# The first feed-forward product as seven half-size products, in a one-core block with three mixers

## The chip, the cores and the metric

The kernel runs on one core of one Trainium2 chip. The metric is device time in microseconds of one launch, the median of several runs.

## The reference, cut to what matters

One residual layer over 512 tokens of width 1024: three token mixers (gated DeltaNet, stick-breaking attention, gated short convolution), merged and projected, then a feed-forward part. All of it is float32. The change is in the feed-forward part:

```python
x = x + rms_norm(merged @ w_out[l], norm_mix_post[l])
h = rms_norm(x, norm_ffn_pre[l])                        # 512 x 1024
f = jnp.square(jax.nn.relu(h @ w_ff1[l])) @ w_ff2[l]    # 1024 -> 4096 -> 1024
x = x + rms_norm(f, norm_ffn_post[l])
```

## The kernel before, in words

**Precision.** Every matmul operand is split into a high part (rounded on ScalarE) and a low part (what remains, subtracted on VectorE), and a product takes three matmuls: high by high, high by low, low by high (`mm3`, L179). Weights come in units of 128 x 1024 numbers, 512 KB: a load on SP's queue into `raw`, a cast on ScalarE (L143), a subtraction on VectorE (L144), into one of three `hl` buffers. These steps are given an earlier place in the order than the work around them (`early`), and each load follows the load before (`lastw`).

**Order.** The program is written out by hand and a planner orders each engine's instructions by the given priorities. First come the projections (`proj`, one weight unit and 24 matmuls each), with the mixers' work put between them by `tick`. Then the output projection, with `out_norm` for each of the four token blocks (residual, norms, `x1` stored in DRAM for later) and `out_transpose`, which puts the normed block on its other axis, as high and low part `h2h`, `h2l`.

**First feed-forward product.** 32 columns of 128 outputs, each with 24 matmuls of 128 x 128 by 128 x 512 (`ff1_mm`). The first three columns are done in token halves, because the last two blocks are not transposed yet. `ff1_act` makes ReLU on ScalarE and multiplies by the sum itself on VectorE, into `aT` (one tile per token half and 256 outputs). `X` and `W` are differences of these tiles, used by the second product.

**Second feed-forward product.** It is already made of seven products of half size each way (Winograd's form of Strassen's scheme), called Q, R, Q, R, S, V, S in the code (`product`), on differences of the activations and on sums of the weights. The weight sums S5, S6 and S1 (8 units each) are made in DRAM, during earlier stages, by `presum`: one call issues on SP's queue a copy of a unit from DRAM to DRAM, and on GpSimd's queue the addition of another unit to the copy issued two calls earlier (`LAG`). Calls stand behind every second gate of the mixers' merge (4) and behind 24 columns of the first product. The last of the seven products adds a further unit in SBUF: a load on SP's queue into one of eight `ch` slots, then an adding transfer on GpSimd's queue (L988).

**Buffers.** PSUM has 8 banks: five of tag `c`, three of tag `mm`. SBUF has 64 tiles of 128 x 512 (`g2`), two of 16 KB a partition (`h16`, which hold h2h and h2l and later the `ch` slots).

## Time and profile before

| | |
|---|---|
| median of 3 runs | 904.28 us (903.99 to 904.78) |
| the profiled execution | 905.1 us |
| its span, first to last instruction | 903.4 us |
| TensorE, VectorE, ScalarE, GpSimd busy | 885.4, 589.0, 452.1, 105.8 us |
| mean granted clock of TensorE | 0.996 |
| moved by transfers | 137 MB |

The busy time of TensorE counts pipelined matmuls with modelled ends, so it says that TensorE had work, not that it ran at its peak. Times in the rows below are microseconds from the start of the span; the first feed-forward product runs from 564.8 to 742.6 us, the second from there to 893.

### The profile page before, as it was taken

Reading aid. Unit: us, or ns where it says so; the run is one execution under the profiler, and the core shown is the slowest. Engines: PE = TensorE matmul, PEld = TensorE weight load, DVE = VectorE, ACT = ScalarE, POOL = GpSimd, SP = SyncE. Lnnn points to the kernel's source line nnn. Section 1 sums busy time; section 2 is a strip of 40 time slices with the busy share of each in tenths; the row PEclk is TensorE's granted clock in tenths of the full one; section 3 lists DMA queues with packets and bytes.
Section 4 is the critical chain, followed back from the end, with each engine's and each line's share of the span. In section 5 each row is a group of like instructions: output and inputs, shape, how many; then the busy total and the mean of one; then the engine's idle time right before and its main releaser. Section 6 shows DMA issues by size and latency. Waiting matters only on the chain.

```text
span 903.4 us, 11761 instructions
## 1 busy us (share of the span) xinstructions
PE 885.4 (98%) x4224; PEld 736.7 (82%) x4224; DVE 589.0 (65%) x1026; ACT 452.1 (50%) x825; POOL 105.8 (12%) x165
## 2 busy tenths in 40 slices
PE   9999999999999999999999999999999999999996
PEld 7788888877788888888888878988888888888885
DVE  4885678987777659655565546533334459878886
ACT  6556875657787732233344333322223237566562
POOL 1003221010112120200000111011111000000120
PEclk9999999999999999999999999999999999999998
DMA  9322223222113144524243552299999339566692
GB/s 313 125 86 82 70 79 118 73 103 71 68 38 106 50 127 121 162 90 117 70 152 126 173 191 94 98 288 288 284 286 269 122 111 373 187 194 203 190 267 103
DMA packets 41626, 136.97 MB, mean 152 GB/s; under 512 B 5456, under 2 KB 5456, under 8 KB 41184
## 3 DMA queue, kind: packets, MB, share of 16 engines
q1 hardware_dynamic: 34032, 111.24, 35.2%
q0 software_dynamic: 7248, 24.68, 13.0%
q8 instruction: 33, 0.54, 0.2%
q10 hardware_dynamic: 288, 0.30, 0.1%
q14 instruction: 25, 0.20, 0.1%
HBM read 131.48 MB, written 29.88 MB: 179 GB/s over the span
## 4 chain that ended last, share of the span: by engine, by line
PE 83%; DVE 10%; issue 3%; ACT 3%; DMA 1%; POOL 0%; DVEq 0%; POOLq 0%; SPq 0%; ACTq 0%
PE mm L179 51%; PE Q L179 5%; PE R L179 5%; PE po L179 5%; PE S L179 5%; PE psv L179 2%; PE V L179 2%; DVE hl L144 2%; DVE c L682 2%; PE p L179 2%; DVE z L683 1%; DVE XX L513 1%; PE pg L179 1%; DVE XX L507 1%; PE warm L179 1%
## 5 line engine op out<-in xcount | busy, mean ns | idle before, releaser
L179 PE MATMUL mm<-hh,hl 128*128 128x512 f32 x928 | 306.0, 397 | 0.9 <-ACT ct L729 0.9
L143 ACT CAST hl<-raw 128x1024 fp32r<-128x1024 f32 x116 | 111.6, 962 | 217.7 <-PE mm L179 189.0
L144 DVE TENSOR_TENSOR hl<-raw,hl 128x1024 fp32r<-128x1024 f32 x116 | 129.9, 1120 | 138.1 <-ACT hl L143 137.8
L179 PEld LDWEIGHTS mm<-hh,hl 128*128 128x128 f32 x928 | 174.1, 188 | 35.7 <-ACT ct L729 1.3
L179 PE MATMUL mm<-hl,hl 128*128 128x512 f32 x464 | 181.1, 390 | 0.0
L179 PE MATMUL mm<-h2h,hl 128*128 128x512 f32 (+1 forms) x528 | 155.0, 377 | 0.4 <-ACT h2h L187 0.2
L179 PEld LDWEIGHTS mm<-h2h,hl 128*128 128x128 f32 x528 | 97.2, 188 | 18.8 <-ACT h2h L187 0.8
L179 PEld LDWEIGHTS mm<-hl,hl 128*128 128x128 f32 x464 | 87.5, 189 | 16.0
L179 PE MATMUL mm<-h2l,hl 128*128 128x512 f32 (+1 forms) x264 | 99.5, 377 | 0.1
L997 DVE TENSOR_TENSOR hl<-ch,hl 128x1024 fp32r<-128x1024 f32 x53 | 64.6, 1223 | 6.2 <-ACT hl L996 6.1
L179 PEld LDWEIGHTS mm<-h2l,hl 128*128 128x128 f32 x264 | 49.7, 188 | 9.4 <-DVE h2l L188 0.3
L996 ACT CAST hl<-ch 128x1024 fp32r<-128x1024 f32 x53 | 55.3, 1046 | 0.0
L179 PE MATMUL po<-wo,mg 128*128 128x512 f32 x192 | 45.2, 391 | 0.0
L179 PEld LDWEIGHTS po<-wo,mg 128*128 128x128 f32 x192 | 35.8, 188 | 7.9 <-ACT mg L187 0.3
L179 PE MATMUL Q<-hl,ahi 128*128 128x512 f32 x128 | 39.7, 391 | 0.0
L179 PE MATMUL R<-hl,ahi 128*128 128x512 f32 x128 | 39.4, 389 | 0.0
L168 POOL DMA_DIRECT2D S<-wst x24 | 20.0, 832 | 151.9 <-DMA S<-wst 115.4
L179 PE MATMUL S<-hl,ahi 128*128 128x512 f32 x120 | 37.0, 389 | 0.0
L682 DVE TENSOR_TENSOR_SCAN c<-c,w 128x512 f32<-128x512 f32 (+3 forms) x32 | 25.5, 815 | 15.1 <-ACT w L106 15.0
L187 ACT CAST ahi<-aT 128x512 fp32r<-128x512 f32 x32 | 19.8, 622 | 28.7 <-PE Q L179 12.1
L179 PEld LDWEIGHTS Q<-hl,ahi 128*128 128x128 f32 x128 | 24.0, 188 | 5.7 <-ACT hl L996 0.4
L947 DVE TENSOR_TENSOR aT<-r,mm 128x256 f32<-128x256 f32 x62 | 23.1, 413 | 7.7 <-ACT r L942 7.7
(297 smaller groups left out, 1448.7 us busy)
## 6 DMA issues: line engine op xcount, KB each, us to landing
raw<-wst SPq DMA_DIRECT2D x92, 512.0 KB, 3.3
ch<-S SPq DMA_DIRECT2D x32, 512.0 KB, 4.3
raw<-wst SPq DMA_DIRECT2D x48, 256.0 KB, 3.2
S<-wst POOLq DMA_DIRECT2D x24, 512.0 KB, 8.7
ch<-wst SPq DMA_DIRECT2D x21, 512.0 KB, 5.2
S<-wst SPq DMA_DIRECT2D x16, 512.0 KB, 8.6
S<-S SPq DMA_DIRECT2D x8, 512.0 KB, 8.7
ch<-wst POOLq DMA_DIRECT2D x8, 512.0 KB, 8.7
```

The lines of the kernel that those rows point to most:

```text
L143: nc.scalar.copy(hl[:, 0, :], raw)
L144: nc.vector.tensor_tensor(hl[:, 1, :], raw, rf(hl[:, 0, :]), ALU.subtract)
L168: nc.gpsimd.dma_start(t, wsrc(1024, *key), accum_op=ALU.add, max_dma_last_dim=4096)
L179: return nc.tensor.matmul(o, l, r, start=start, stop=stop, skip_group_check=more)
L187: nc.scalar.copy(hi, src)
L507: nc.vector.tensor_tensor(tmp[:, :, :w], X[:, :, j].unsqueeze(2).to_broadcast([P, 8, w]), L[:, j, j + 1:].unsqueeze(1).to_broadcast([P, 8, ...
L513: nc.vector.tensor_tensor(X[:, :, j + 1:], X[:, :, j + 1:], tmp[:, :, :w], ALU.subtract)
L682: nc.vector.tensor_tensor_scan(back, back, w[j][:, ks][:, ::-1], 0.0, ALU.add, ALU.add)
L683: nc.vector.tensor_tensor(z[j][:, :n], z[j][:, :n], c[j][:, :n], ALU.subtract)
L947: x = nc.vector.tensor_tensor(aT[i][u][:, f % 2, :], r[:, c], ps[:, c], ALU.mult)
L996: after[0] = nc.scalar.copy(hl[0][:, c], r)
L997: after[1] = nc.vector.tensor_tensor(hl[1][:, c], r, rf(hl[0][:, c]), ALU.subtract)
```

## The change

**The first product** becomes seven products of half size: tokens in halves, the 1024 inner numbers in halves (k), the 4096 outputs in halves (n). For each group u of 256 outputs there are M1 to M7, each 24 matmuls of 128 x 128 by 128 x 256 with one weight unit. The left operands are the quarters A(i, q) of h2 (token half i, inner half q) and four combinations X, Y, Z, W, made by `combine` on VectorE after the transposes and split in high and low parts. On the right, M2, M3 and M4 use plain units, M5 and M6 use the sums F5 and F6, made in DRAM by `presum`; M1 uses F5 plus one more unit, added in SBUF in one of two buffers, and M7 adds another unit to the sum that M1 left there. The results are added and subtracted on VectorE (`step`) and then go through ReLU and square as before.

**The order.** The lead is M5 of groups 0 and 1, which needs the plain quarter A(0, 0) only, then M3, M2, M1, M4, M6, M7 of both groups with the transposes of the last two token blocks in between. Groups 2 to 7 follow one after the other.

**Weight sums.** There are 32 sums in DRAM instead of 24: F5 and F6 are new, S1 goes. The calls of `presum` now stand in every second projection, but not while `quiet` is set (parts of the triangular inverse, and from the last gates to the output projection), and in every fourth of the seven-product steps. In the second feed-forward product the S product adds its second unit in SBUF slots, and the last product adds one more unit to these slots in place; V uses other buffers.

**Other.** `x1` is stored from GpSimd's queue instead of SP's.

```diff
-    S5, S6, S1 = ([dp.tile([P, 1024], F32, tag=f"{n}{u}", bufs=1, name=f"{n}{u}") for u in range(8)]
-                  for n in ("S5", "S6", "S1"))
+    def sums(which, n):
+        return [dp.tile([P, 1024], F32, tag=f"{which}{n}{u}", bufs=1, name=f"{which}{n}{u}") for u in range(8)]
...
+    def plan(t, of, plus):
...
+    def f1(k, n):
...
+    def f2(k, n):
...
+    F5, F6, S5, S6 = (sums(w, n) for w in "FS" for n in (5, 6))
+    plan(F5, f1(1, 1), f1(0, 1))
+    plan(F6, f1(0, 0), f1(0, 1))
+    plan(S5, f2(1, 1), f2(0, 1))
+    plan(S6, f2(0, 0), f2(0, 1))
+    quiet = [False]
+    calls = [0]
...
     def presum():
+        if quiet[0]:
+            return
...
     def proj(c0, x=False):
+        calls[0] += 1
+        if calls[0] > 2 and calls[0] % 2:
+            presum()
...
     def gdn_inverse(h0):
+        quiet[0] = True
...
+        quiet[0] = False
         for j in range(31):
+            quiet[0] = j >= 16
...
+        quiet[0] = False
...
-        if dm % 2 == 1:
-            presum()
...
+    quiet[0] = True
...
-    h2h = hp.tile([P, KT, T], F32R, tag="h16", name="h2h")
-    h2l = hp.tile([P, KT, T], F32R, tag="h16", name="h2l")
...
+    FB, op = {}, {}
+    homes = [hp.tile([P, 4, 4, 256], F32R, tag="h16", name=nm("h2")) for _ in range(2)]
+    for j, (p_, q_) in enumerate(((("A", 0, 0), "X"), (("A", 1, 0), ("A", 1, 1)))):
+        op[p_] = [[homes[j][:, e, 2 * g:2 * g + 2, :] for g in range(2)] for e in range(2)]
+        op[q_] = [[homes[j][:, 2 + e, 2 * g:2 * g + 2, :] for g in range(2)] for e in range(2)]
...
-            nc.sync.dma_start(x1d[b, hf], x1[hf])
+            nc.gpsimd.dma_start(x1d[b, hf], x1[hf])
...
     def out_transpose(b, h2):
-        bs = slice(b * P, b * P + P)
+        i, ts_ = b // 2, slice(b % 2 * P, b % 2 * P + P)
         for q in range(2):
             pt = bank("pt")
             for j in range(4):
                 nc.tensor.transpose(pt[:, j * P:j * P + P], h2[q][:, j * P:j * P + P], ident)
             p3 = pt.rearrange("p (k c) -> p k c", k=4)
-            split(h2h[:, q * 4:q * 4 + 4, bs], h2l[:, q * 4:q * 4 + 4, bs], p3)
+            if b % 2 == 0:
+                FB[i, q] = [g2("F", F32, (P, 2, 256)) for _ in range(2)]
+            if (i, q) == (0, 0):
+                split(homes[0][:, 0, :, ts_], homes[0][:, 1, :, ts_], p3)
+            elif i == 1:
+                split(homes[1][:, 2 * q, :, ts_], homes[1][:, 2 * q + 1, :, ts_], p3)
+            for g in range(2):
+                nc.scalar.copy(FB[i, q][g][:, :, ts_], p3[:, 2 * g:2 * g + 2, :])
+        if b % 2 == 0:
+            return
+        if i == 0:
+            FB["X"] = [g2("X", F32, (P, 2, 256)) for _ in range(2)]
+            combine("X", FB["X"], FB[0, 1], FB[0, 0])
+        else:
+            combine("Y", FB["X"], FB[1, 1], FB["X"])
+            combine("Z", FB[1, 0], FB[1, 0], FB["X"])
+            combine("W", FB[0, 1], FB[0, 1], FB[1, 1])
+    def combine(name, o, a=None, b=None):
+        if name not in op:
+            op[name] = [[g2("op", F32R, (P, 2, 256)) for _ in range(2)] for _ in range(2)]
+        for g in range(2):
+            if a is not None:
+                nc.vector.tensor_tensor(o[g], a[g], b[g], ALU.subtract)
+            split(op[name][0][g], op[name][1][g], o[g])
...
+    NR = 3
+    raws = [[(slice(0, 512), g2("rw")), (slice(512, 1024), g2("rw"))] for _ in range(NR)]
...
-    def ff1_mm(w, ps, ts_):
...
+    big = []
+    def slot(n):
+        if not big:
+            for _ in range(2):
+                t = hp.tile([P, 4, 1024], F32, tag="h16", name=nm("ch"))
+                big.extend([(all_, t[:, i, :])] for i in range(4))
+        return big[n % 8]
+    def right(src, raw, plus=None, second=True):
+        if raw is None:
+            raw = [(all_, wp.tile([P, 1024], F32, tag="raw", bufs=2, name=nm("raw")))]
...
-            lastw[0] = x
+            if src is not None:
+                x = nc.sync.dma_start(r, src[:, c])
+                dep(x, lastw[0])
+                lastw[0] = x
             if plus is not None:
                 nc.gpsimd.dma_start(r, plus[:, c], accum_op=ALU.add)
...
-    def block(k, n):
-        return lambda u: wsrc(1024, "ff2", n, 8 * k + u)
+    def block(k, n, slots):
+        return lambda u: (wsrc(1024, *f2(k, n)(u)), slots(u))
+    def m2_slot(u):
+        return raws[(2, 0, 1)[u]] if u < 3 else slot(u - 3)
+    m2_block = block(0, 0, m2_slot)
...
+    wsum = {"M1": F5, "M5": F5, "M6": F6, "M2": f1(0, 0), "M3": f1(1, 1), "M4": f1(1, 0)}
+    more = {"M1": f1(0, 0), "M7": f1(1, 0)}
+    left = {"M1": "Y", "M2": ("A", 1, 0), "M3": "X", "M4": ("A", 1, 1), "M5": ("A", 0, 0), "M6": "Z", "M7": "W"}
+    done = [0]
+    def ff1_product(m, ps, u, first):
+        done[0] += 1
+        if done[0] > 5 and done[0] % 4 == 0:
             presum()
...
+        if m in more:
+            raw = raws[u % 2]
+        else:
+            raw = (None, None, raws[2])[turn["r"] % 3]
+            turn["r"] += 1
+        b = wsum.get(m)
+        src = None if b is None else b[u] if isinstance(b, list) else wsrc(1024, *b(u))
+        with early():
+            w = right(src, raw, wsrc(1024, *more[m](u)) if m in more else None, False)
+        hi, lo = op[left[m]]
+        for j in range(2):
+            o = ps[:, j * 256:j * 256 + 256]
+            for k in range(4):
+                c = slice(k * 256 + j * P, k * 256 + j * P + P)
+                xh_, xl_ = hi[k // 2][:, k % 2, :], lo[k // 2][:, k % 2, :]
+                mm(o, w[0][:, c], xh_, first and j == 0 and k == 0, False, True)
+                mm(o, w[0][:, c], xl_, False, False, True)
+                mm(o, w[1][:, c], xh_, False, k == 3, True)
...
+    def step(m, u):
+        lead = u < 2
+        if m == "M1":
+            ff1_product(m, bank_for("S", u, mbank), u, True)
+            if lead:
+                d = flat(aT[1][8 + u])
+                tt(d, d, pb["S", u], ALU.add)
+            else:
+                nc.scalar.copy(new(1, 8 + u), pb["S", u])
+        elif m == "M5" and lead:
+            ff1_product(m, bank_for("R", u, mbank), u, True)
+            nc.scalar.copy(new(1, 8 + u), pb["R", u])
+        elif m == "M3":
+            if not lead:
+                bank_for("R", u, mbank)
+            ff1_product(m, pb["R", u], u, not lead)
+            d = flat(aT[1][8 + u])
+            if lead:
+                tt(d, pb["R", u], d, ALU.subtract)
+                relu2(new(0, 8 + u), pb["R", u])
+            else:
+                tt(d, d, pb["R", u], ALU.add)
+        elif m == "M2":
+            ff1_product(m, bank_for("Q", u, lambda: bank("Q")), u, True)
+            d = flat(aT[1][8 + u])
+            tt(d, d, pb["Q", u], ALU.subtract)
+        elif m == "M5":
+            ff1_product(m, pb["R", u], u, False)
+            relu2(new(0, 8 + u), pb["R", u])
+        elif m == "M4":
+            ff1_product(m, pb["Q", u], u, False)
+            g = new(0, u)
+            tt(g, flat(aT[1][8 + u]), pb["Q", u], ALU.add)
+            tt(g, g, pb["R", u], ALU.subtract)
+            relu2(new(1, u), pb["Q", u])
+        elif m == "M6":
+            ff1_product(m, bank_for("V", u, lambda: bank("V")), u, True)
+            d = flat(aT[1][8 + u])
+            tt(d, d, pb["V", u], ALU.add)
+            if u == 7:
+                ready.append(unit(A10, m2_block, 0))
+            relu2(d, d)
+        else:
+            ff1_product(m, bank_for("T", u, lambda: bank("T")), u, True)
+            g = flat(aT[0][u])
+            tt(g, g, pb["T", u], ALU.add)
+            if u == 7:
+                ready.append(unit(A10, m2_block, 1))
+            relu2(g, g)
+            X.append(g2("X", F32, (P, 2, 256)))
+            tt(flat(X[-1]), flat(aT[0][8 + u]), g, ALU.subtract)
+            W.append(aT[0][8 + u])
+            tt(flat(W[-1]), flat(W[-1]), flat(aT[1][8 + u]), ALU.subtract)
+    quiet[0] = False
+    step("M5", 0)
+    step("M5", 1)
+    out_transpose(2, h2s[2])
+    step("M3", 0)
+    out_transpose(3, h2s[3])
+    step("M3", 1)
+    for m, u in (("M2", 0), ("M2", 1), ("M1", 0), ("M1", 1), ("M4", 0), ("M6", 0), ("M4", 1), ("M7", 0), ("M6", 1),
+                 ("M7", 1)):
+        step(m, u)
+    for u in range(2, 8):
+        for m in ("M1", "M3", "M2", "M5", "M4", "M6", "M7"):
+            step(m, u)
...
+    for tb in product(Q, A10, m2_block, True):
...
+    for tb in product(R, lambda u: X[u], block(1, 1, lambda u: slot(5 + u)), True):
...
+    for tb in product(Q, lambda u: A[1, 1][u], block(1, 0, lambda u: slot(13 + u)), False):
...
+    for tb in product(R, lambda u: A[0, 0][u], lambda u: (S5[u], slot(21 + u)), False):
...
-    for tb in product(S, lambda u: sub(A[1, 1][u], X[u], X[u]), lambda u: S1[u], True):
+    for tb in product(S, lambda u: sub(A[1, 1][u], X[u], X[u]), lambda u: (S5[u], slot(29 + u), wsrc(1024, *f2(0, 0)(u))), True):
...
-    for tb in product(V, lambda u: sub(A[1, 0][u], X[u], X[u]), lambda u: S6[u], True):
+    for tb in product(V, lambda u: sub(A[1, 0][u], X[u], X[u]), lambda u: (S6[u], raws[u % 3]), True):
...
-    for tb in product(S, lambda u: W[u], lambda u: (S1[u], block(1, 0)(u)), False, 2):
+    for tb in product(S, lambda u: W[u], lambda u: (None, slot(29 + u), wsrc(1024, *f2(1, 0)(u))), False, 2):
...
         if kind == "ff1":
-            return cols(w_ff1, i[0] * P)
+            return cols(w_ff1[512 * i[0]:512 * i[0] + 512], 2048 * i[1] + 256 * i[2], 256)
         return cols(w_ff2[256 * i[1]:256 * i[1] + 256], i[0] * 512, 512)
```

## Rows read from the trace of the kernel before

**Rows 1.** The page's engine totals: busy us, share of the span, instructions.
```profile
PE 885.4 (98%) x4224; PEld 736.7 (82%) x4224; DVE 589.0 (65%) x1026; ACT 452.1 (50%) x825; POOL 105.8 (12%) x165
```

**Rows 2.** The chain that ended last, in time order: start us, us, what.
```profile
557.15 0.87 PE pt L898 x8
...
571.68 2.76 PE f L179 x23
...
584.82 157.79 PE mm L179 x696
```

**Rows 3.** Windows: window and length, busy us (instructions) per engine, granted clock, DMA share, GB/s.
```profile
584.80:742.60 157.80, 157.80 (x698) 130.69 (x697) 65.37 (x106) 46.03 (x62) 19.67 (x26) 1.00 0.82 235
742.60:765.00 22.40, 22.40 (x99) 17.93 (x98) 19.98 (x26) 15.57 (x22) 1.08 (x2) 1.00 0.99 385
830.00:852.00 22.00, 22.00 (x99) 18.22 (x98) 20.38 (x27) 13.42 (x19) 0.13 (x1) 1.00 0.60 197
```

**Rows 4.** Groups by form on VectorE: busy us, mean ns, idle before and its releaser.
```profile
L997 DVE TENSOR_TENSOR hl<-ch,hl 128x1024 fp32r<-128x1024 f32 x53 | 64.6, 1223 | 6.2 <-ACT hl L996 6.1
...
L890 DVE SCALAR_TENSOR_TENSOR h<-x,st,wff 128x512 f32<-128x512 f32 x8 | 5.7, 749 | 2.0 <-POOL st L850 2.0
...
L952 DVE TENSOR_TENSOR X<-aT,aT 128x512 f32<-128x512 f32 x8 | 5.5, 684 | 0.0
L188 DVE TENSOR_TENSOR h2l<-pt,h2h 128x512 fp32r<-128x512 f32 x8 | 5.3, 681 | 4.9 <-ACT h2h L187 4.9
...
L997 DVE TENSOR_TENSOR hl<-rw,hl 128x512 fp32r<-128x512 f32 x6 | 3.9, 682 | 0.0
```

**Rows 5.** Groups by form on ScalarE, in the same columns.
```profile
L996 ACT CAST hl<-ch 128x1024 fp32r<-128x1024 f32 x53 | 55.3, 1046 | 0.0
...
L942 ACT ACTIVATE r<-mm 128x512 f32<-128x512 f32 x31 | 18.4, 593 | 10.5 <-issue 10.5
...
L187 ACT CAST ah<-at 128x256 fp32r<-128x256 f32 x8 | 3.1, 385 | 0.0
```

**Rows 6.** Windows with a lone copy, DRAM addition, and load; then additions into SBUF.
```profile
276.00:279.00 3.00, 3.00 (x18) 2.66 (x17) 1.23 (x4) 2.19 (x5) 0.95 (x3) 1.00 0.76 262
282.00:285.00 3.00, 2.18 (x13) 1.62 (x12) 2.90 (x7) 2.38 (x5) 0.00 (x0) 1.00 1.04 177
286.50:289.00 2.50, 2.17 (x14) 1.85 (x13) 2.22 (x6) 1.50 (x3) 1.69 (x2) 1.00 0.64 210
...
852.00:884.00 32.00, 32.00 (x143) 26.51 (x142) 26.65 (x33) 19.81 (x28) 7.33 (x9) 1.00 0.99 246
```

**Rows 7.** Window of the first product with all weight sums in flight, same columns.
```profile
590.00:700.00 110.00, 110.00 (x487) 91.13 (x486) 41.61 (x66) 31.80 (x41) 16.58 (x21) 1.00 1.01 284
```

**Rows 8.** Transfers issued from 590 to 700 us: count, KB each, median us to landing.
```profile
raw<-wst SPq DMA_DIRECT2D x20, 512.0 KB, 7.9
S<-wst POOLq DMA_DIRECT2D x19, 512.0 KB, 8.9
S<-wst SPq DMA_DIRECT2D x9, 512.0 KB, 9.0
S<-S SPq DMA_DIRECT2D x8, 512.0 KB, 8.7
```

**Rows 9.** Transfers issued from 852 to 874 us, in the same columns.
```profile
ch<-wst POOLq DMA_DIRECT2D x7, 512.0 KB, 8.4
ch<-S SPq DMA_DIRECT2D x6, 512.0 KB, 8.5
```

**Rows 10.** The page's costliest groups: GpSimd issuing the DRAM additions.
```profile
L168 POOL DMA_DIRECT2D S<-wst x24 | 20.0, 832 | 151.9 <-DMA S<-wst 115.4
```

**Rows 11.** Window in the middle of the projections, columns as in Rows 3.
```profile
140.00:300.00 160.00, 153.46 (x780) 128.47 (x779) 129.94 (x250) 116.61 (x221) 18.45 (x33) 0.99 0.23 73
```

**Rows 12.** Timeline at the change of stages: start us, us, instruction, idle before and releaser.
```profile
562.50 0.54 POOL L850 TENSOR_TENSOR st<-st,half 128x1 f32<-128x1 f32 x1 [2.59 <-DVE st L849]
...
564.83 0.50 PE L179 MATMUL mm<-h2h,hl 128*128 128x256 f32 x2
```

More of the change, by code (lines that the diff above doesn't have):

```diff
@@ L934, in trunk_kernel @@
     flat = lambda t: t.rearrange("p j c -> p (j c)")
-    def ff1_act(f, ps):
-        u = f // 2
-        if f % 2 == 0:
-            for i in range(2):
-                aT[i].append(g2("aT", F32, (P, 2, 256)))
-        r = sm.tile([P, 512], F32, tag="r", bufs=2, name=nm("r"))
-        x = nc.scalar.activation(r, ps, AF.Relu)
-        if ready:
-            dep(x, after[0])
-        for i in range(2):
-            c = slice(i * 256, i * 256 + 256)
-            x = nc.vector.tensor_tensor(aT[i][u][:, f % 2, :], r[:, c], ps[:, c], ALU.mult)
-            if ready:
-                dep(x, after[1])
-        if f % 2 == 1 and u >= 8:
-            X.append(g2("X", F32, (P, 2, 256)))
-            nc.vector.tensor_tensor(flat(X[-1]), flat(aT[0][u]), flat(aT[0][u - 8]), ALU.subtract)
-            W.append(aT[0][u])
-            nc.vector.tensor_tensor(flat(W[-1]), flat(W[-1]), flat(aT[1][u]), ALU.subtract)
-    lead = [(wnext("ff1", f), mbank()) for f in range(2)] + [(wnext("ff1", 2), bank("f1"))]
-    for i, (w, ps) in enumerate(lead):
-        ff1_mm(w, ps, slice(0, 256))
-        if i > 0:
-            out_transpose(i + 1, h2s[i + 1])
-    for f, (w, ps) in enumerate(lead):
-        ff1_mm(w, ps, slice(256, 512))
-        ff1_act(f, ps)
-    NJ, NR = 4, 3
+    for i in range(2):
+        aT[i].extend([None] * 16)
+    NJ = 4
     stats = [(g2("ahi", F32R, (P, 2, 256)), g2("alo", F32R, (P, 2, 256))) for _ in range(NJ)]
-    raws = [[(slice(0, 512), g2("rw")), (slice(512, 1024), g2("rw"))] for _ in range(NR)]
     turn = {"s": 0, "r": 0, "w": 0}
@@ L971, in ring @@
         return of[(turn[what] - 1) % len(of)]
-    def right(src, plus=None):
-        if turn["r"] < NR:
-            raw = ring("r", raws)
-        else:
-            if turn["r"] == NR:
-                raws.clear()
-                for _ in range(2):
-                    t = hp.tile([P, 4, 1024], F32, tag="h16", name=nm("ch"))
-                    raws.extend([(slice(0, 1024), t[:, i, :])] for i in range(4))
-            raw = ring("r", raws)
+    all_ = slice(0, 1024)
+    big = []
[8 more added lines that the diff above has]
+            raw = [(all_, wp.tile([P, 1024], F32, tag="raw", bufs=2, name=nm("raw")))]
         for c, r in raw:
-            x = nc.sync.dma_start(r, src[:, c])
-            dep(x, lastw[0])
-            lastw[0] = x
+            if src is not None:
+                x = nc.sync.dma_start(r, src[:, c])
+                dep(x, lastw[0])
+                lastw[0] = x
             if plus is not None:
                 nc.gpsimd.dma_start(r, plus[:, c], accum_op=ALU.add)
-        turn["w"] += 1
-        if turn["w"] % 4:
+        turn["w"] += second
+        if not second or turn["w"] % 4:
             hl = wp.tile([P, 2, 1024], F32R, tag="hl", bufs=3, name=nm("hl"))
@@ L1009, in unit @@
         with early():
-            src = block(u)
-            return stat(left(u)), right(*src) if isinstance(src, tuple) else right(src)
+            return stat(left(u)), right(*block(u))
     A10 = lambda u: aT[1][u]
-    for f in range(3, 30):
-        if f >= 6:
-            presum()
-        w = wnext("ff1", f)
-        ps = mbank()
-        ff1_mm(w, ps, slice(0, 512))
-        ff1_act(f, ps)
-    late = [(wnext("ff1", 30), mbank())]
-    ff1_mm(*late[0], slice(0, 512))
-    late.append((wnext("ff1", 31), mbank()))
@@ L1024, in trunk_kernel @@
-    ready.append(unit(A10, block(0, 0), 0))
-    ff1_act(30, late[0][1])
-    ff1_mm(*late[1], slice(0, 512))
-    ready.append(unit(A10, block(0, 0), 1))
-    ff1_act(31, late[1][1])
+    wsum = {"M1": F5, "M5": F5, "M6": F6, "M2": f1(0, 0), "M3": f1(1, 1), "M4": f1(1, 0)}
[5 more added lines that the diff above has]
+        if done[0] > 5 and done[0] % 4 == 0:
+            presum()
+        if m in more:
[16 more added lines that the diff above has]
+                mm(o, w[1][:, c], xh_, False, k == 3, True)
@@ new lines, in new, with relu2, tt, bank_for @@
+    def new(i, f):
+        aT[i][f] = g2("aT", F32, (P, 2, 256))
+        return flat(aT[i][f])
+    def relu2(o, src):
+        r = sm.tile([P, 512], F32, tag="r", bufs=2, name=nm("r"))
+        x = nc.scalar.activation(r, src, AF.Relu)
+        if ready:
+            dep(x, after[0])
+        x = nc.vector.tensor_tensor(o, r, src, ALU.mult)
+        if ready:
+            dep(x, after[1])
+    def tt(o, a, b, op_):
+        nc.vector.tensor_tensor(o, a, b, op_)
+    pb = {}
+    def bank_for(m, u, where):
+        pb[m, u] = where()
+        return pb[m, u]
```

17 lines of the change are left out of this document (3 added, 14 removed).

## The prediction

> **What bounds the kernel now.** I read the page's engine totals first: TensorE is busy 98% of 903.4 us, VectorE 65%, ScalarE 50% [rows 1]. The chain of waits in order of time then says whether that is matmul time or waiting. In the first feed-forward product it is one piece of 696 matmuls in 157.79 us with nothing in between [rows 2]. TensorE alone sets the time there, so a matmul taken out is time won, as long as nothing else becomes late. The windows say what else could. While the product of 584.8 to 742.6 us runs, VectorE works 65.4 of 157.8 us and ScalarE 46.0, so both have much to give; the transfers have less, a share of 0.82 over the stage [rows 3]. The second feed-forward product is already built of half-size products, and there VectorE works 20.38 of 22 us while TensorE loses nothing [rows 3]: 93% is the fullest VectorE that this trace shows to be harmless.
>
> **What is removed: matmul time.** A 512-column matmul takes 157.79/696 = 226.7 ns. A 256-column one takes 2.76/23 = 120 ns [rows 2], not half of it: 13.3 ns of each do not shrink with the columns. The first product now has 29 x 24 = 696 wide matmuls and, for its three leading columns done in token halves, 3 x 24 x 2 = 144 narrow ones: 157.8 + 17.3 = 175.1 us. After the change it has 7 products x 8 column groups x 24 = 1344 narrow ones: 161.3 us. An eighth of the multiplications goes, and the extra starts eat a third of that: **13.8 us gained**. The stage ran from 564.83 us [rows 12] to 584.82 + 157.79 = 742.61 us, 177.8 us; 1.8 us of it are two groups of eight transposes at 0.87 [rows 2], which stay, and 0.9 us waits. Without new waits it would last 164.0 us.
>
> The Trainium skill, "TensorE: Matmul & The Clock Gate", section "Back-to-back issue gap", gives N/2.4 + 2.5 ns per warm matmul, 215.8 and 109.2 ns. By it the stage would go from 165.9 to 146.8 us, 19.1 us gained. The rows have 226.7 and 120 at a granted clock of 1.00 [rows 3], so the sum goes by them.
>
> **What is added: VectorE and ScalarE.** A unit of weights used to serve 24 matmuls of 226.7 ns, 5.44 us; now it serves 24 x 0.12 = 2.88 us. Every unit costs one cast on ScalarE (1.05 us) and one subtraction on VectorE: 1.223 us in one piece, 2 x 0.682 = 1.364 in two halves [rows 4, 5]. M1 and M7 always use buffers of two halves, and the other five products one time in three. That is 3.67 x 1.364 + 3.33 x 1.223 = 9.1 us of VectorE for the seven units of a column group. What follows each product is 128x512 work on VectorE at 0.69 us [rows 4]: one operation after M3 and M2, none after M1 (a ScalarE copy), one after M5, three after M4, two after M6, four after M7: 12 x 0.69 = 8.3 us. A group costs VectorE 17.4 us against 7 x 2.88 = 20.2 us of matmuls, 86%. ScalarE has 7 casts of about 1.1, four ReLUs and a copy of 0.6 [rows 5]: 11 us. It has room.
>
> The lead is worse. It has 14 products (two groups, 40.3 us of matmuls and 1.8 of transposes). VectorE has in it: 11 weight subtractions (three units are split before) 14.4 us; the four combinations X, Y, Z, W, each two differences and two low parts, 16 x 0.69 = 11.0; five low parts of h2 at 0.68, 3.4; what is left of the last token block's norm, one product, two additions and two scalings at 0.75 and two small steps [rows 4], 4.1; and 26 operations behind the products, 17.9. That is 50.8 us for 42.1. Some of it may be done late, what follows M7 above all. But M1 of group 0 is the seventh product, 6 x 2.88 + 1.8 = 19.1 us after the first starts, and before it VectorE owes 0.68 (a low part) + 4.1 (the norm) + 2.76 (X) + 2.72 (four low parts) + 5.17 (four weight units) + 2.76 (M3, twice) + 0.69 (M2) + 2.76 (Y) = 21.6 us. ScalarE owes about as much there: twelve copies of 256-column pieces at 0.385 [rows 5], casts, squares. So TensorE waits at least **2.5 us** in the lead.
>
> The whole stage asks of VectorE 50.8 + 6 x 17.4 + 4.1 (the first two units of the next product) - 2.8 (what follows the last M7) = 156.5 us, 95% of 164. At the 93% that was harmless it needs 168.3: **4.3 us** more. The bounds of this term are nothing (VectorE can be filled to 95%) and some 12 us (89%, which is what it showed at 742.6 to 765 us [rows 3], with each step of subtract, ReLU, multiply in order, so that VectorE waits 0.6 us for ScalarE four times per group). I take the middle one because the pattern of these windows, two splits per unit, is the nearest to the new stage. The cover of all this work is the matmuls alone.
>
> **Transfers.** Alone, a weight load holds the engines 0.64 x 2.5 = 1.6 us, a copy from DRAM to DRAM 2.3, an addition into DRAM 3.1 [rows 6]. In full queues they overlap: 385 GB/s is 1.36 us per 512 KB load [rows 3]. From 590 to 700 us, 20 loads and some 18 copies with their additions filled 110 us at share 1.01 without delaying a matmul [rows 7, 8]: (110 - 27)/18 = 4.6 us per precomputed sum. From 852 to 884 us 7.9 MB moved, of which 8 additions into SBUF and the rest like 7 loads: (31.7 - 9.5)/8 = 2.8 us per addition [rows 6]. The new stage has six loads and two additions into SBUF per group, 48 x 1.36 + 16 x 2.8 = 110 us. (M7 adds to what M1 left in its buffer and loads nothing.) Of the 32 sums that go to DRAM (24 before), I count 21 calls that come in the projections, 25 odd ones less about four in quiet stretches, so some 11 to 12 remain for this stage: 53 us. Together 163 us, 12 of them (five loads, two additions) ahead of the stage: 151 of 164, nearly full but not over. I charge nothing for throughput; the latency of one chain is a rival, below.
>
> The 17 additional sums in the projections cost GpSimd 0.83 us of issue each [rows 10]. From 140 to 300 us TensorE does wait for VectorE and ScalarE, but GpSimd works only 18.5 of 160 us and the transfers have a share of 0.23 [rows 11], so a weight load behind a copy still lands early. I charge **0.5 us**; the bounds are 0 and 8 (ten of them, each 0.8 us in front of a masking step that everything waits for). Storing x1 from GpSimd's queue costs nothing: its two issues, 1.7 us at 0.83, lie in the 2.6 us in which GpSimd waits for the second sum of squares [rows 12]. In the second product the multiplications stay; its S sums are now a load plus an addition in slots that are free eight units, 21.8 us, earlier, and the W sums are added in place with a whole product (21.8 us) between. 16 additions x 2.8 + 16 loads x 1.36 = 67 us within three products, 65 us, with the first ready before: at zero, up to 4 us if late.
>
> **The sum.** -13.8 + 2.5 + 4.3 + 0.5 = -6.5 us. The profiled execution took 905.1 us with a span of 903.4; 898.6 follows. It lay 0.8 us over the median of the runs, 904.28: **897.8 us**.
>
> **Rivals.** *All hidden* (22%): work that can slip fills VectorE to 95% and the lead's lateness is absorbed by three weight buffers. Then -13.8 + 0.5: 891 us. For it speaks the second product, where VectorE at 93% cost nothing; against it that there TensorE seldom waits for what VectorE makes of TensorE's own results.
>
> *The sum for M1 comes late* (25%), which ends at no change or slower. Sync issues loads in order, and M6's load waits until M2's weights have been split, at the earliest 2.3 us into M1 of the same group. M1's load of the next group stands behind it, then the addition, then a cast and two subtractions, 2.0 us. From there to M1's start remain 20.2 - 2.3 - 2.0 = 15.9 us. In full queues a load landed after 8.5 us and an addition after 8.4 [rows 9], with 0.83 to issue: 17.7 us, 1.8 late, six times 10.8 us. VectorE's later loss hides inside, so -13.8 + 2.5 + 10.8 + 0.5 = 0.0, 904.3 us. It is slower than before by 0.2% once the sum takes 18.0 us (six times 2.1, 906.1); at 19 us the time is 912. Against it: the stage's queues are a little less full than those rows, and alone a load holds the engines for 1.6 us only and an addition for 3.1 [rows 6].
>
> The Trainium skill, "DMA: Bandwidth & Descriptors", section "Anatomy of one DMA", has about 2 us + bytes/436 GB/s for a transfer issued from GpSimd, 3.2 us here; by it the sum would be there in 7 us and this rival void. The rows' 8.4 us say otherwise for additions in full queues.
>
> *The projections pay* (9%): the extra sums hold up GpSimd or a weight load between 140 and 440 us, 0.8 us ten times: -7.0 + 8, 905.3 us, more if VectorE is also late.
>
> *A matmul costs its columns and nothing else* (2%): a narrow one takes half of 226.7 ns, 113.3, and the 1344 take 152.3 us, 9 less than in my sum: 889 us. The 23 narrow ones of the lead contradict it [rows 2]. It is close to the rule of the Trainium skill quoted above.
>
> **Chances.** The forecast, 893.5 to 902, has 42%. A median can tell from no change what is over 0.2%, 1.8 us. Faster: 42 + 22 + 2 + 2 (M1 late by little) = 68%; same: 10 of M1 late and 2 of the projections, 12%; slower: 13 + 7 = 20%. The range leaves out a tenth at each end: below 889.5 lies little but the fourth rival, above 908 the late M1 at over 18.3 us. The likeliest case alone spans 893.5 to 902.
>
> **What would show it.** In the profile after: 1344 narrow matmuls at 120 ns and a stage of 168 to 172 us instead of 177.8; VectorE at 90 to 95% in it; TensorE's waits in its first 30 us ending at VectorE's low parts of Y, Z or W, or at ScalarE's casts; later ones at weight subtractions. If instead the waits end at an addition into M1's buffer once per group, the late sum is right. Transfers should be near full to about 720 us, and the second product still at 21.76 us each. The prediction is wrong if narrow matmuls run at another rate, or if TensorE waits before 528 us grow.

## The result, and the profile after

The changed kernel takes 949.25 us (947.35 to 950.92, 4 runs); the kernel before took 904.53 on the same chip (903.99 to 905.19, 4 runs). The ratio is 1.049, 95% interval 1.047 to 1.052: slower by 5%, where 897.8 was forecast and 908 was the end of the range. The profiled execution took 950.1 us, span 948.2. The page's engine totals:

```profile
PE 895.2 (94%) x4728; PEld 763.9 (81%) x4728; DVE 657.9 (69%) x1119; ACT 492.9 (52%) x916; POOL 152.3 (16%) x221
```

TensorE has 9.8 us more work than in [rows 1] and 35 us more time without work. The starts of the stages, read from TensorE's timeline, say where (us; FF1 and FF2 are the two feed-forward products, "lead" the first two column groups of FF1 up to M1 of group 2, the rest six groups of seven products; Q, R, S, V are products of FF2, two further ones of 21.8 us are left out):

| kernel | first FF1 matmul | lead | six groups | FF1 | first Q | first R | S | V | last | span |
|---|---|---|---|---|---|---|---|---|---|---|
| before | 564.8 | | | 177.6 | 22.2 | 21.8 | 21.8 | 21.8 | 29.9 | 903.4 |
| after | 569.0 | 59.2 | 147.2 | 206.4 | 28.1 | 21.8 | 21.8 | 28.3 | 29.4 | 948.2 |

Of 44.8 us, 28.8 lie in FF1, 5.9 in Q, 6.5 in V and 4.2 ahead of FF1. Windows of the lead, the groups, Q, V and the projections, in the columns of [rows 3]:

```profile
569.00:628.20 59.20, 48.55 (x351) 46.64 (x349) 41.77 (x66) 28.38 (x55) 13.65 (x17) 0.91 0.79 212
628.20:772.50 144.30, 128.52 (x986) 123.86 (x985) 98.08 (x141) 62.67 (x97) 26.01 (x30) 0.96 0.87 226
775.40:803.40 28.00, 24.94 (x98) 19.64 (x97) 21.60 (x29) 15.77 (x22) 0.00 (x0) 0.88 0.71 267
890.50:918.80 28.30, 25.05 (x98) 17.57 (x97) 15.26 (x24) 12.60 (x21) 3.08 (x6) 1.00 0.83 245
140.00:300.00 160.00, 149.78 (x742) 125.77 (x741) 127.76 (x241) 111.99 (x212) 24.98 (x41) 0.97 0.45 127
```

In the groups VectorE works 68% of the time, not 90 to 95%, and the transfers are not full either (a share of 0.87): nothing is at its limit, so this is a chain of waits. The narrow matmuls came as forecast: a product of 24 follows the next at 2.88 us. The waits from 560 to 775 us (engine, line, what ended them: us, times, longest), Sync's queue last:

```profile
ACT hl L1019 <- DMA rw<-wst: 53.8, 16, 9.2
...
POOL rw L1011 <- DVE hl L1020: 39.0, 12, 9.4
POOL rw L1011 <- DMA rw<-F: 38.8, 7, 14.0
...
PE mm L193 <- ACT hl L1019: 13.4, 8, 4.4
```
```profile
SPq L1007 <- DVE hl L1020: 150.5, 44, 16.1
```

And the chain that ended last, from the third group on (start us, us, what):

```profile
634.32 1.22 DVE hl L1020 x2
636.07 6.04 DMA rw<-F
643.29 11.26 DMA rw<-wst
654.57 0.63 ACT hl L1019
...
661.58 6.50 DMA S<-wst
669.88 10.31 DMA rw<-wst
680.21 0.63 ACT hl L1019
```

Read from the top: VectorE splits a weight unit and so frees a buffer; only then does Sync, which issues in order, get to the load of M1's copied sum (rw<-F, 6.0 us); then GpSimd's addition (rw<-wst, 11.3 us); then the cast. The first half of M1 starts at 653.25 and its second half waits. The next round ends 25.6 us later, and the six groups take 25.0, 26.4, 24.9, 26.8, 21.4 and 22.6 us. Ahead of M1, TensorE's wait ends at a cast that stood for the addition into M1's buffer in four of the six groups: the sign that the prediction named for this rival. These waits are 7.2 us of the 26 that the groups lose against 20.2 each. Another 8.5 end at VectorE, which has just stood idle for the same cast (5.8 us before 653.23) and then has its work all at once. The remaining 10 are matmuls that took longer behind the waits, at a mean granted clock of 0.96.

The second round passes through GpSimd's queue: the copy for a later sum (S<-wst) leaves Sync just ahead of M1's load, and the addition that waits for it stands ahead of M1's. It cost next to nothing there, since by the landings in the trace M1's own load came 0.6 us after the copy.

### The profile page after: what moved, and what is told of

It reads as the page before. It is cut to its first block, busy times and chain, and to the rows that moved or that the text cites. A ratio compares the mean times of both kernels' runs of the same rounds, so it can differ in the third digit from the quotient of the medians.

```text
span 948.2 us, 13161 instructions
## 1 busy us (share of the span) xinstructions
PE 895.2 (94%) x4728; PEld 763.9 (81%) x4728; DVE 657.9 (69%) x1119; ACT 492.9 (52%) x916; POOL 152.3 (16%) x221
## 4 chain that ended last, share of the span: by engine, by line
PE 37%; DMA 19%; DVE 13%; issue 10%; ACT 4%; POOL 2%; SPq 0%; DVEq 0%; POOLq 0%; ACTq 0%
PE mm L193 21%; DMA rw<-wst 8%; PE Q L193 5%; PE R L193 3%; DMA rw<-S 2%; DMA rw<-F 2%; DVE hl L1020 2%; PE S L193 2%; DMA ch<-wst 2%; DMA S<-wst 2%; DVE hl L144 2%; PE p L193 2%; DVE c L703 1%; DVE aT L1086 1%; DVE aT L1081 1%
## 5 line engine op out<-in xcount | busy, mean ns | idle before, releaser
L143 ACT CAST hl<-raw 128x1024 fp32r<-128x1024 f32 x84 | 77.8, 926 | 109.2 <-PE mm L193 83.9
L1019 ACT CAST hl<-rw 128x512 fp32r<-128x512 f32 x80 | 47.2, 617 | 95.3 <-DMA rw<-wst 53.8
L1020 DVE TENSOR_TENSOR hl<-rw,hl 128x512 fp32r<-128x512 f32 x80 | 52.8, 687 | 61.5 <-ACT hl L1019 61.5
L193 PE MATMUL mm<-h,hl 128*128 128x256 f32 x384 | 51.7, 291 | 9.5 <-ACT hl L1019 4.4
L193 PEld LDWEIGHTS mm<-h,hl 128*128 128x128 f32 x384 | 48.8, 197 | 11.7 <-ACT hl L1019 4.6
L193 PE MATMUL Q<-h,hl 128*128 128x256 f32 x384 | 51.0, 290 | 5.1 <-ACT hl L1019 2.9
L193 PEld LDWEIGHTS Q<-h,hl 128*128 128x128 f32 x384 | 49.1, 198 | 5.5 <-ACT hl L1019 5.5
L193 PE MATMUL mm<-op,hl 128*128 128x256 f32 x192 | 33.9, 331 | 11.8 <-ACT hl L1019 9.0
L1011 POOL DMA_DIRECT2D rw<-wst x32 | 28.9, 967 | 98.2 <-DVE hl L1020 39.0
L193 PEld LDWEIGHTS mm<-op,hl 128*128 128x128 f32 x192 | 29.5, 229 | 15.9 <-ACT hl L1019 10.6
```

Source lines behind the costliest of these rows:

```text
L143: nc.scalar.copy(hl[:, 0, :], raw)
L193: return nc.tensor.matmul(o, l, r, start=start, stop=stop, skip_group_check=more)
L1011: nc.gpsimd.dma_start(r, plus[:, c], accum_op=ALU.add)
L1019: after[0] = nc.scalar.copy(hl[0][:, c], r)
L1020: after[1] = nc.vector.tensor_tensor(hl[1][:, c], r, rf(hl[0][:, c]), ALU.subtract)
```

## The experiments

Four theories. A: the load for M1 leaves too late, since Sync's order puts it behind loads that wait for splits. B: GpSimd's queue, held at its head by an addition whose copy has not landed. C: the amount of data moved. D: VectorE's work. The table at the end of this section has the stages of all runs. A run with one time is a single execution.

**M1's load early** (M7's addition issued with M1's product, M1's load and addition a group ahead of its use; the code is shortened).
```
+    def ahead(m, u):
+        if (m, u) == ("M5", 1): sum_load("M1", 0); sum_load("M1", 1)
+        if m == "M1": sum_load("M7", u)
+        if (m, u) == ("M6", 1): sum_load("M1", 2)
+        if m == "M5" and 2 <= u < 7: sum_load("M1", u + 1)
```


> The same work as the changed kernel, but the load and the addition for M1 of a group are issued right after M5's load of the group before, and M7's addition right after M1's weights are split. Theory A (the sum for M1 is late because its load stands behind M6's and M2's on Sync's queue and its two landings follow one another): the first product falls from 204.8 us to 170 to 180 and the time from 949 to 915 to 925 us. Theory B (additions into DRAM stand in front on GpSimd's queue and wait for their copies): 195 to 200 us, time 940 to 945. Theory C (the transfers are simply too many for the stage): no change, 200 to 205 us. Theory D (VectorE, the forecast): no change either.

922.1 us; FF1 179.3 instead of 206.4. The same transfers and the same instructions, issued in another order, give back 27 us of the 28.8. The window of the groups:

```profile
618.70:743.70 125.00, 120.21 (x987) 118.71 (x986) 97.05 (x140) 62.95 (x97) 26.12 (x30) 1.00 0.96 261
```
The transfers are now fuller (0.96 against 0.87), and TensorE loses 5 us instead of 16. So full transfers alone do not set the time, and GpSimd's waits for copies do not either: they are 53.0 us in this run's FF1, more than the 45.3 of the changed kernel. What counts is when M1's sum is there, as A says; but the run moves the additions on GpSimd's queue as well as the load on Sync's.

**All sums in DRAM made in the projections** (four calls between copy and addition; none left for FF1).
```
-        if calls[0] > 2 and calls[0] % 2:
+        if calls[0] > 2:
-        if done[0] > 5 and done[0] % 4 == 0:
-            presum()
```


> All 32 sums in DRAM are made in the projections, one call in every projection and with four calls instead of two between a copy and its addition; none is left in the first product. Theory B: the additions for M1 and M7 are issued at once, the first product falls to 170 to 185 us. Theory C: about 53 of the 163 us of transfers leave the stage, it falls to 170 to 180 us. Theory A: landings get shorter by 2 to 4 us each, but the order of loads is the same: 185 to 195 us. The stretch before it, 570.6 us in the changed kernel, stays the same or gets 0 to 5 us shorter if what held it up was an addition that waited for its copy, and longer by 5 us or more if it was the transfers themselves.

931.2 us: FF1 178.4, but its first matmul comes at 576.6. Sync's order of loads in FF1 is as in the changed kernel, and for that theory A expected 185 to 195 us: it missed. With the sums gone from the stage the additions for M1 and M7 land sooner (the changed kernel above, this run below):

```profile
rw<-wst POOLq DMA_DIRECT2D x32, 256.0 KB, 8.3
rw<-wst POOLq DMA_DIRECT2D x32, 256.0 KB, 5.3
```

That shortens M1's chain enough (its first group took 22.9 us, the others 20.2 to 20.9). So the lateness has two ingredients, a late start and slow landings, and taking away either one is nearly enough. The sums cost the projections 7.6 us more instead, against the changed kernel's profile.

**Plain weights for M1, M5, M6 and M7** (leaves out all weight sums of the first product; every matmul and split stays).
```
-    plan(F5, f1(1, 1), f1(0, 1))
-    plan(F6, f1(0, 0), f1(0, 1))
+    wsum = {"M1": f1(0, 0), "M5": f1(1, 1), "M6": f1(0, 0), "M7": f1(1, 0), ...
```


> Leaves out the sums of weights in the first product: M1, M5, M6 and M7 take plain units, nothing is added in DRAM or SBUF for them, and the 16 sums of the second product are made before the first. Theories A, B and C: the whole excess of the first product goes, 164 to 168 us instead of 204.8. Theory D: VectorE's work is all there, so the stage stays at 171 us or above, with VectorE at 91% or more.

916.0 us. Windows of the lead and of the groups:

```profile
566.60:619.00 52.40, 45.06 (x351) 44.08 (x350) 46.36 (x72) 30.88 (x59) 2.22 (x4) 0.93 0.46 161
619.00:740.00 121.00, 121.00 (x1010) 121.00 (x1010) 98.44 (x140) 61.88 (x96) 0.00 (x0) 1.00 0.53 180
```
In the groups TensorE never stops, with all of VectorE's work there (81%): D falls for the groups. FF1 as a whole takes 173.4 us, where A to C expected 164 to 168 and D 171 or more; the difference is all in the lead. It still takes 52.4 us, with a transfer share of 0.46 against 0.79: its loss is not the sums.

**Eight pairs of buffers for V's weights, not three.**
```
+    vraw = raws + [[...g2("rw")..., ...g2("rw")...] for _ in range(8 - 3)]
-    (S6[u], raws[u % 3])
+    (S6[u], vraw[u % 8])
```


> V in the second product gets eight weight buffers instead of three. If V waits because only three loads can be under way while each takes 9 to 13 us to land, V takes 21.8 us again and the time falls by 6 to 7 us, to about 943 us. If it waits because the additions for the last product take the transfer engines, V's loads land later still and it stays within 2 us of 949.

950.9 us, V 28.6: the number of buffers is not what V waits for.

**Additions four calls behind their copies**, alone.
```
-    LAG = 2
+    LAG = 4
```


> The changed kernel with one number changed: an addition in DRAM is issued four calls after its copy and not two. If GpSimd's queue, held at its head by an addition whose copy has not landed, is what costs the projections, the first matmul of the first product comes back from 569.0 to 565 to 567 us; if the amount of data moved is, it stays at 568 to 570. In the first product the groups are set by the order of the loads of M1 (first theory): 200 to 208 us as before, 945 to 948 in all. If the additions that wait on GpSimd's queue set them (second theory), the stage falls below 195 us, in all below 938.

944.3 us; first matmul at 563.5, FF1 203.9. The edit did not reach the chip as meant. In this trace every engine has its instructions in the same order as in the changed kernel, and GpSimd still waits for a copy eight times in FF1 (the changed kernel above, this run below):

```profile
POOL S L182 <- DMA S<-wst: 45.3, 8, 11.5
POOL S L182 <- DMA S<-wst: 46.9, 8, 11.4
```

Nor do the additions stand two calls behind their copies in the kernel before, whatever its code says: by the landings in its trace all 24 leave 0.3 to 0.6 us after their own copy has landed. In the run with all sums in the projections, which has the same edit, they follow at once too. So this run is the changed kernel once more. It says nothing of B, which no run took alone; against B stand the 53.0 us of such waits with M1 early and the landings in the result above. What the run does give is the scatter of one program: 5 us in all, 5.6 in the start of FF1, 2.4 in FF1. Twelve runs of this study have the changed kernel's order up to 555 us; they start FF1 at 563.5 to 569.0, mean 566.4.

**Q's weights in freed slots from unit 2 on** (with M1 early).
```
-        return raws[(2, 0, 1)[u]] if u < 3 else slot(u - 3)
+        return raws[(2, 0)[u]] if u < 2 else slot(u - 2)
```


> The kernel with M1's load early, and product Q of the second product takes its weights into the freed slots from unit 2 on, where it took them from unit 3 on; unit 2 no longer waits for the buffer that the first product's last M7 splits. If that one buffer holds Sync's queue at the handover, Q falls from 28.6 us to 22 to 24 and the whole to 915 to 917 us. If the slow start of Q comes from the transfers or from the clock that fell after the first product, Q stays at 27 to 29 us and the whole at 921 to 923.

920.0 us, Q 29.0: a miss. ScalarE's timeline at the handover shows the reason:

```profile
738.76 0.59 ACT L1099 ACTIVATE r<-Q 128x512 f32<-128x512 f32 x1
742.43 1.05 ACT L1019 CAST hl<-ch 128x1024 fp32r<-128x1024 f32 x1 [3.07 <-DMA ch<-wst]
743.38 0.61 ACT L201 CAST ahi<-aT 128x512 fp32r<-128x512 f32 x1
```
The cast of a weight (hl<-ch, in the order of the instructions that of unit 3) stands in front of the left side that Q needs first (ahi), and waits 3.07 us for its transfer. VectorE's work is late by as much, and TensorE pauses 2.70 us at 750.7. The rest of the loss is the clock (TensorE's timeline, then a window):

```profile
753.36 2.08 PE L193 MATMUL Q<-hl,ahi 128*128 128x512 f32 x4 [2.70 <-ACT ahi L201]
```
```profile
754.00:760.00 6.00, 6.00 (x15) 4.27 (x14) 3.10 (x6) 1.20 (x2) 0.00 (x0) 0.52 0.34 117
```
After that pause the granted clock is 0.52, the lower level of 1.2 GHz, and 15 matmuls take the time of 26.

**Left sides of Q's units 2 and 3 split ahead of their weights**, on the same kernel.
```
+            if turn["w"] in (3, 4):
+                dep(after[0], sa[0])
+                dep(after[1], sa[1])
```


> The kernel of the slots run (M1 early, Q's weights in slots from unit 2 on) with two orders fixed on ScalarE and VectorE: the splits of the left side of Q's units 2 and 3 come ahead of the splits of their weights. If the handover is lost because ScalarE stands for 3.07 us at the split of a later unit whose weights have not landed, with Q's first left split behind it, Q falls from 29.0 us to 22 to 24 and the whole from 920 to 913 to 916. If VectorE's backlog (full from 748 to 754 with the evacuations of the last two products) is what holds Q, the order changes little: Q 27 to 29, the whole 918 to 921.

915.7 us; Q 23.6 instead of 29.0: the order of two engines was 5.4 us of Q's loss of 6.7.

**S without its eight additions** (leaves out half of S's weight sum; M1 early).
```
-    (S5[u], slot(29 + u), wsrc(1024, *f2(0, 0)(u)))
+    (S5[u], slot(29 + u))
```


> The kernel with M1's load early, without the eight additions in SBUF for product S (it leaves out half of S's weight sum). If the sixteen additions of S and of the last product together fill the transfer engines while V's weights are loaded, V falls from 28.5 us to 22 to 24, the whole to 915 to 917 us. If V is late for another reason (its three pairs of buffers, the reloads of x1 on GpSimd's queue), V stays at 27 to 29 and the whole at 921 to 923.

915.3 us; V 21.8, with the transfers of its window at a share of 0.54 instead of 0.83:

```profile
862.00:883.80 21.80, 21.80 (x98) 18.06 (x97) 15.73 (x24) 13.16 (x22) 0.00 (x0) 1.00 0.54 178
```
In the changed kernel the queues from 856 to 915 us held S's and W's additions (14.2 us from issue to landing), V's loads and the reloads of x1 at once:
```profile
ch<-wst POOLq DMA_DIRECT2D x13, 512.0 KB, 14.2
rw<-S SPq DMA_DIRECT2D x16, 256.0 KB, 13.5
x1a<-x1d POOLq DMA_DIRECT2D x8, 256.0 KB, 15.2
```
Here, in one place, C is the cause: without S's eight additions V loses nothing. What the reloads of x1 add to it no run took apart.

**M1 early, Q's slots, S's sums again in DRAM, and the splits of M3 ahead of the copies and subtractions for Y, Z, W** (Q's order is not in it).
```
+    plan(S1, S5, f2(0, 0))      # and a call of presum() per unit of FF2
+                if b >= 2: dep(x, head[b - 2][0])
```


> All repairs together: M1's load early, additions four calls behind their copies, Q's weights in slots from unit 2 on, S's sums again made in DRAM (eight copies and eight additions, issued in products Q and R), and the splits of M3's first two weight blocks put ahead of the copies and subtractions for Y, Z and W. By the stages of the runs so far: first matmul 565.5, first product 179.3 less 4 for the lead, Q 22, four products of 21.8, V 22, the rest 29.5: a span of 901 us and 903 in all (range 899 to 910), so at the time of the kernel before. If the sums in DRAM fill the transfers of Q and R in their turn, one of these takes 25 us or more and the whole is 907 to 912; if the lead is not held by the two engines' order, it stays at 51 us and the whole is 907.

925.1 us (ratio 1.024, 1.021 to 1.028) where 903 was expected: worse than its parts. V is 21.8, but Q 35.0: in the trace the copies for S, issued at the handover, stand between Q's loads on Sync's queue, and Q's loads take 20.4 us to land by the median (6.7 with M1 early alone). M1's first unit came 22.5 us into the lead instead of 28.4, yet the lead took 51.2 and the first group 28.8 (24.8 with M1 early alone): M1's third unit waited 2.1 us for a sum whose load needs the buffer that M7's first split frees.

**Three pairs of buffers for M1 and M7, S's copies from R on, Q's order** (M3's splits not moved); then the same **with M3's splits moved**.
```
-            raw = raws[u % 2]
+            raw = raws3[u % 3]
```


> M1 and M7 take turns on three pairs of buffers instead of two, so the load for M1's third unit stands behind no split of M7; with it M1 early, additions four calls behind, Q's weights in slots with its splits in order, and S's sums in DRAM, made from product R on. If the change's loss is latency in the two in-order queues and nothing else, the lead falls from 51.4 us to 46 to 48, the first group from 24.8 to 20.2, and the stages add up to 564 + 171 + 22.5 + 4 x 21.8 + 21.8 + 29.5 = 896 of span, 898 in all (range 893 to 904): faster than the kernel before. If the transfers of the first product are full whatever the order (its additions and copies), the groups stay above 21 us each and the whole is 905 to 912.

> As the run with three pairs, and the splits of M3's first two weight blocks ahead of the copies and subtractions for Y, Z and W on ScalarE and VectorE. In the run with all earlier repairs the matmuls reached M1's first unit 22.5 us after the first one and not 28.4, and lost it again at M1's third unit, whose load waited for a buffer. With that buffer free the lead is 43 to 46 us and the whole 3 to 5 us below the run with three pairs alone: 894 us (range 889 to 902). If the lead's time is set by the amount of splits on the two engines, it comes to the same time as that run, within 1 us.

916.5 us (1.014, 1.011 to 1.017) and 910.3 (1.008, 1.005 to 1.010), where 898 and 894 were expected. The third pair brings the first group to 20.2 us. In the second run the first four groups take 20.2 us each, with the transfers at shares of 0.99 to 1.06 from 630 to 710 us. The lead is 53.9 and 53.8, so the forecasts of 43 to 48 were wrong: in the second the time won at M3 is lost again before M1's second unit, which needs a bank that VectorE has not cleared:

```profile
587.72 3.04 PE L194 MATMUL mm<-op,hl 128*128 128x256 f32 x24
595.50 4.40 PE L194 MATMUL mm<-op,hl 128*128 128x256 f32 x24 [4.74 <-DVE aT L1129]
```

**M4's first unit ahead of M1's second**, and then **four of S's sums in DRAM, four in SBUF**.
```
-    ("M1", 0), ("M1", 1), ("M4", 0), ...
+    ("M1", 0), ("M4", 0), ("M1", 1), ...
+    (S5[u], slot(30 + u), wsrc(...)) if u < 4 else (S1[u], slot(30 + u))
```


> As the run with the lead's splits moved and three pairs, with one order changed in the lead: M4's first unit stands before M1's second. In that run TensorE waited 4.74 us ahead of M1's second unit for VectorE to clear a bank; M4's first unit needs no new bank. If the bank is what the lead waits for, it falls from 53.8 to 48 to 50 us, and the whole by as much, to 904 to 906. If the lead is set by VectorE's total (it worked without a pause from 579 to 595), the wait moves to the weights of the next unit and the lead stays at 52 to 54, the whole at 908 to 911.

> As the run before it, with four of S's eight sums made in DRAM and four by additions in SBUF. With eight in DRAM, R lost 2.7 us with the transfer engines at share 1.04; with eight in SBUF, V lost 6.7. If it is only the sum of transfers in a stretch that counts, four and four fit on both sides: R and V both at 22 to 23, the whole 2 to 3 us below the run before it. If one side is still too full, R or V stays at 24 or more and the whole is the same as the run before it.

913.5 us (1.011, 1.010 to 1.013), 3 us more than the run before it although the lead is 1.7 us shorter, 52.1: the wait only moved on, and R took 26.0. TensorE's timeline there, in the later of the two runs:

```profile
591.21 0.50 PE L194 MATMUL Q<-h,hl 128*128 128x256 f32 x2 [1.31 <-ACT hl L1028]
593.42 0.47 PE L194 MATMUL mm<-op,hl 128*128 128x256 f32 x2 [1.70 <-DVE aT L1129]
594.46 4.33 PE L194 MATMUL Q<-h,hl 128*128 128x256 f32 x22 [0.57 <-DVE hl L1029]
```
With four and four, R is back at 21.8 and V stays there: 905.9 us (903.0 to 908.9, 12 runs), against 903.9 before (17 runs), ratio 1.002, 1.001 to 1.004. Its lead and groups:
```profile
564.30:615.70 51.40, 45.05 (x352) 43.62 (x351) 46.09 (x72) 31.01 (x59) 15.81 (x21) 0.97 0.95 252
615.70:742.40 126.70, 122.64 (x1010) 121.24 (x1009) 95.82 (x138) 62.07 (x96) 24.05 (x28) 1.00 0.96 266
```

| run | us | first FF1 matmul | lead | FF1 | first Q | first R | V |
|---|---|---|---|---|---|---|---|
| M1 early | 922.1 | 567.3 | 51.4 | 179.3 | 28.6 | 21.8 | 28.5 |
| sums in projections | 931.2 | 576.6 | 54.0 | 178.4 | 28.6 | 21.8 | 28.4 |
| plain weights | 916.0 | 566.6 | 52.4 | 173.4 | 28.7 | 21.8 | 28.6 |
| eight pairs for V | 950.9 | 566.3 | 59.5 | 207.6 | 30.0 | 21.8 | 28.6 |
| four calls behind | 944.3 | 563.5 | 58.9 | 203.9 | 29.9 | 21.8 | 28.5 |
| slots | 920.0 | 565.1 | 51.8 | 178.9 | 29.0 | 21.8 | 28.7 |
| S without additions | 915.3 | 567.5 | 51.7 | 179.0 | 28.4 | 21.8 | 21.8 |
| Q's order | 915.7 | 566.8 | 50.6 | 176.8 | 23.6 | 21.8 | 30.1 |
| M3's splits, S in DRAM | 925.1 | 567.5 | 51.2 | 182.6 | 35.0 | 21.8 | 21.8 |
| three pairs, Q's order | 916.5 | 567.3 | 53.9 | 181.2 | 23.7 | 23.3 | 21.8 |
| and M3's splits | 910.3 | 565.2 | 53.8 | 177.1 | 23.1 | 24.5 | 21.8 |
| and M4 ahead | 913.5 | 567.1 | 52.1 | 179.2 | 23.1 | 26.0 | 21.8 |
| and four and four | 905.9 | 564.3 | 51.4 | 178.1 | 23.3 | 21.8 | 21.8 |

## Why the prediction was wrong

**The step that failed** is the wait for M1's weight sum. The forecast's sum charged nothing for it and kept it as the rival *the sum for M1 comes late*, with 25% and 10.8 us. It happened, and cost some 34 us: 26 in the six groups (147.2 us against 6 x 20.2 = 121) and 8 in the lead (59.2 against 51.4 with the load early). The load and addition were priced nearly right together, 17.7 us against 6.04 + 1.2 + 11.26 = 18.5 in the round shown, though by two errors that cancel: the load took 6.0 us and not 8.5, the addition 11.3 and not 8.4. Wrong was the time that they have. The working let the load leave 2.3 us into M1 of the group, "at the earliest" M2's split. In the trace M1 of group 2 starts at 628.2 and the next load at about 636, 7.8 us in, and the later ones leave 4.9 to 8.9 us in: Sync's queue has come no further, because it waits for VectorE's splits, which stand behind ScalarE's casts, which wait for the last addition. (The total of 150.5 us of such waits proves nothing by itself: Sync waits 79.0 us in the same way before the change, and 132.3 with M1 early.) An earliest time was used for a link of a loop whose own delay feeds back.

That the lateness of M1's sum is the cause is shown from three sides. FF1 gets back 27 us when M1's load and additions are issued earlier, 28 when no sum is made in DRAM during FF1, and 33 when there are no sums. How much of it is Sync's order and how much the slow landings stays open, since either repair alone is nearly enough.

**Matmul time** (-13.8 us) was right: 2.88 us per product, and six groups of 20.2 us when nothing is late (the plain weights).

**VectorE.** The 4.3 us for filling it over the whole stage were wrong in the groups (81% busy, no loss). They belong to the lead, and there far more: the working found 50.8 us of VectorE for 42.1 of matmuls and charged 2.5, since some of it may be done late. The lead took 50.6 to 54.0 us in all eleven runs in which M1's sum was early, unhurried or absent, through three changes of order in it; in the last, VectorE works 46 of 51.4 us. So 50.8 was close to the lead itself, but that may be luck: with M1 early alone VectorE works only 41.4 us in the lead, and it takes the same 51.4. That VectorE's total decides is argued from the wait that moved; no run took work off VectorE in the lead. One part was left out of the working: with the pauses the granted clock of the last run's lead is 0.97, and TensorE works 45.1 us there where 42.1 were counted.

**Transfers in FF1**, charged nothing: at shares of 0.95 to 1.06 the groups take 20.2 us in some runs and 21.1 in the last, up to 6 us in all. Whether those 6 us are the transfers is not shown. As an ingredient of M1's chain, above, they counted for more.

**Projections**, charged 0.5 us: FF1 starts 1.6 us later by the mean of the twelve runs than in the one profile of before, within their scatter of 5.6; open. The prediction's sign was that TensorE's waits before 528 us grow, and they did a little: 12.8 us without work in the changed kernel and 11.0 in its second launch, against 9.7 before. Moving all the sums there is clearly dear (7.6 us above the latest start of the twelve).

**The second product**, charged nothing with a bound of 4 us: 12.4 measured, in two ways. V lost 6.5 us to transfers, the "67 us within three products, 65 us" that the working called harmless: 67 is already more than 65, and the reloads of x1 were left out of that sum. Q lost 5.9 to an order of splits that the working did not look at; 5.4 of it came back with the order.

In the last run, with all these repairs, the six groups win 6.5 us (126.7 against three quarters of before's 177.6) and the lead gives back 7.0 (51.4 against a quarter): FF1 takes 178.1 us, and the kernel is 0.2% slower than the one before, 0.1 to 0.4% by the interval. No version of the study beats it.

## What to carry to other kernels

Where a buffer's chain (free, load, add, split, use) closes on itself once per iteration, add up the whole loop, queue waits included, against the iteration; the earliest time of one link says little. Two repairs were worth the same here: to issue the load and addition an iteration ahead, and to take other transfers out of their way. When products get cheaper, cost the start-up by itself: it can lose time even if the steady state has room. Sum the transfers of a crowded stretch with everything that is prefetched into it. And read in the trace whether an experiment's edit changed the order that the engines got: one of those above did not, and its difference of 5 us was scatter.

## What the runs showed of the hardware

An addition from DRAM into 256 KB of SBUF took 8.2 to 11.3 us to land on the chain that ended last in the groups (8.3 by the median of all 32 in FF1, 5.3 with no sums made beside them), where the load before it took 6.0, and a 512 KB one 14.2 by the median in the stretch from 856 us. A pause of 2.70 us at the start of Q cost about as much again: the granted clock of the six microseconds behind it was 0.52. The 24 matmuls behind the pause of 4.74 us in the lead took 4.40 us, where 24 in an unbroken row take 3.04 in the same columns. The start of FF1 scattered by 5.6 us over twelve runs with the same order of instructions ahead of it; a single run against another says nothing about less.
